# Two context norms made one part sooner, and the second layer's first weights behind the last g, in a two-layer trunk kernel on one core

## The chip, the cores and the metric

The kernel runs on one core of a Trainium2 chip. Its engines each work through a queue of their own, in order: TensorE (PE, matmuls, with PEld for its weight loads), VectorE (DVE), ScalarE (ACT), GpSimd (POOL) and SyncE (SP, which issues DMAs). The metric is the device time of one execution in microseconds (us), lower is better.

## What is computed

The reference is a trunk of two layers over 512 latent tokens x and 256 context tokens c, model width 1024. Layer 0 mixes differential attention and neighbourhood attention, layer 1 is windowed grouped-query attention; each is followed by a SwiGLU FFN. In front of each of the four sub-layers stands a modulated RMS norm, behind each a gated residual add, with separate modulation rows for x and for the context:

```python
def rmsnorm(x, g):
    xf = x.astype(jnp.float32)
    y = xf * lax.rsqrt(jnp.mean(xf * xf, axis=-1, keepdims=True) + NORM_EPS)
    return (y * g.astype(jnp.float32)).astype(x.dtype)

def modulate(h, shift, scale):
    return h * (1 + scale) + shift

def swiglu(h, w1, w3, w2):
    return (jax.nn.silu(h @ w1) * (h @ w3)) @ w2
```

## The kernel before

Everything lies with the model dimension on the 128 partitions: the residual of x is eight tiles `xr[k]` of 512 columns, that of the context eight tiles `cr[k]` of 256. Every operand is kept as a high and a low half, and each product is three matmuls per 128 rows: weight high by h high (L207), weight high by h low (L208), weight low by h high (L209); the FFN's pair products and its down projection do the same on L1233 to L1235 and L1265 to L1267. A weight comes as one DMA of 512 KB from SP into one of three raw buffers. Its halves are made in one of two ways: ACT copies the high half and DVE subtracts (`split`, and L158 and L159 for plain weights), or ACT writes the negated weight, POOL issues a DMA that accumulates the raw weight onto it, and ACT copies the high half (`split_by_dma`).

A norm is a chain over four engines: eight squares on ACT (L329, L332), summed in two accumulators by DVE (L338) and POOL (L336); matmuls with a matrix of ones that sum over the partitions (L309, in `rstd_of`); logarithm, exponential and a Newton step on ACT and DVE (L313 to L318); then for each k the normed and modulated h, DVE (L350), ACT (L351, its high half) and DVE (L352, its low half), in `h_make`. The h's go to `hb[k]`, x columns and context columns apart (`hx`, `hc`). The norm takes its small tiles from a pool or from a `Carve`, which cuts them out of one big tile.

The first attention (until about 478 us) ends with the output projection, whose last context parts are `held` back behind the start of the x norm of the first FFN. The first FFN (478 to 1023 us) begins with `plain_tile(0)`, one hidden tile of 128 columns: two weights by x and by the context, then Silu on ACT, a product on DVE, and the split into `g`. In it `between()`, which is `norm_c`, traces the context norm behind the first x product. `keep_busy` issues 16 matmuls of no use ahead of it. Three more plain tiles follow, then pairs of hidden tiles by a scheme of seven products on token sums (`token_sums`, `seven`). The last pair's down projection is `down_last`: four parts of w2, x columns first (512 wide, eight output tiles m), then the context's 256 columns m by m; behind context m = 2 stands `next_norm`, the x norm of the second attention. The rows of the modulation are made beside this on DVE from streamed weights (L269, L270). The second attention begins with `k_x(0)`, the first K product of x; the context norm of this layer is traced behind it, then V of x and of the context, K of the context, and `k_x(1)`.

What sets the order: the code is traced in this order, and a scheduler then orders each engine's queue by a simulated timeline of its own; `tc.issue_after(a)` holds an instruction behind a in the order. Weights are taken from the stream `S` by `S.next`, which makes the halves of some parts ahead of their use.

## Time and profile before

| what | us |
|---|---|
| median of the runs shown (1660.72 to 1665.11) | 1663.11 |
| the profiled execution | 1662.13 |
| its span | 1660.3 |
| PE busy in the span | 1573.4 |
| DVE busy | 1255.2 |
| ACT busy | 754.0 |
| POOL busy | 270.1 |
| mean granted clock of TensorE | 0.988 |

The profiled execution lies 1.0 us below the median, and 1.8 us of it lie outside the span. PE is busy in 95% of the span, and the chain of work that ended last is PE in 61%. A granted clock of 1.00 is 2.4 GHz, 0.50 is 1.2 GHz; a number between them in a window is a mean of the two.

### The profile page before, as it was taken

Reading aid. Unit: us, or ns where it says so; the run is one execution under the profiler, and the core shown is the slowest. Engines: PE = TensorE matmul, PEld = TensorE weight load, DVE = VectorE, ACT = ScalarE, POOL = GpSimd, SP = SyncE. Lnnn points to the kernel's source line nnn. Section 1 sums busy time; section 2 is a strip of 40 time slices with the busy share of each in tenths; the row PEclk is TensorE's granted clock in tenths of the full one; section 3 lists DMA queues with packets and bytes.
Section 4 is the critical chain, followed back from the end, with each engine's and each line's share of the span. In section 5 each row is a group of like instructions: output and inputs, shape, how many; then the busy total and the mean of one; then the engine's idle time right before and its main releaser. Section 6 shows DMA issues by size and latency. Waiting matters only on the chain.

```text
span 1660.3 us, 26333 instructions
## 1 busy us (share of the span) xinstructions
PE 1573.4 (95%) x10220; PEld 1406.1 (85%) x10220; DVE 1255.2 (76%) x2155; ACT 754.0 (45%) x1330; POOL 270.1 (16%) x314
## 2 busy tenths in 40 slices
PE   5899998999998999999999999999999899999996
PEld 3798987877887889999999987777788798989896
DVE  4758698966565988879798868687666797868685
ACT  5445555456245423333434253456654453524343
POOL 2223112454010000010100011254321000000001
PEclk9999999999999999999999999999999999999998
DMA  9312254544124556675766763411011342323321
GB/s 337 111 56 80 77 156 143 180 140 126 56 82 101 149 167 153 165 199 156 193 186 175 197 167 101 99 54 39 14 39 41 114 138 77 117 87 102 115 77 51
DMA packets 69652, 200.05 MB, mean 120 GB/s; under 512 B 6948, under 2 KB 19396, under 8 KB 69528
## 3 DMA queue, kind: packets, MB, share of 16 engines
q1 hardware_dynamic: 59464, 164.40, 31.8%
q0 software_dynamic: 9488, 33.44, 9.3%
q8 instruction: 81, 1.33, 0.3%
q10 hardware_dynamic: 576, 0.52, 0.1%
q14 instruction: 43, 0.35, 0.1%
HBM read 160.45 MB, written 4.86 MB: 100 GB/s over the span
## 4 chain that ended last, share of the span: by engine, by line
PE 61%; DVE 8%; DMA 4%; issue 3%; ACT 2%; POOL 0%; DVEq 0%; SPq 0%; ACTq 0%; POOLq 0%
PE f L1235 4%; PE f L1234 4%; PE f L1233 4%; PE f L1631 4%; PE f L1633 4%; PE f L1632 4%; PE f L1265 3%; PE f L1266 3%; PE f L1267 3%; PE lin L207 2%; PE t L1466 2%; PE lin L208 2%; PE lin L209 2%; PE f L1686 2%; PE f L1684 2%
## 5 line engine op out<-in xcount | busy, mean ns | idle before, releaser
L196 ACT ACTIVATE wh<-raw 128x1024 fp32r<-128x1024 f32 (+1 forms) x94 | 90.2, 976 | 229.3 <-DVE raw L500 121.1
L207 PE MATMUL lin<-hb,wh 128*128 128x512 f32 (+1 forms) x456 | 162.1, 356 | 8.3 <-DVE q L369 2.2
L208 PE MATMUL lin<-hb,wh 128*128 128x512 f32 (+1 forms) x456 | 160.0, 351 | 0.2
L209 PE MATMUL lin<-hb,wl 128*128 128x512 f32 (+1 forms) x456 | 158.9, 349 | 0.0
L197 DVE TENSOR_TENSOR wl<-raw,wh 128x1024 fp32r<-128x1024 f32 (+1 forms) x94 | 104.5, 1116 | 32.5 <-ACT wh L196 31.8
L159 DVE TENSOR_TENSOR wl<-raw,wh 128x1024 fp32r<-128x1024 f32 x64 | 84.3, 1317 | 41.2 <-ACT wh L158 41.0
L1265 PE MATMUL f<-g,wh 128*128 128x512 f32 (+1 forms) x320 | 108.7, 342 | 5.5 <-DVE q L1247 3.9
L269 DVE SCALAR_TENSOR_TENSOR junk<-raw,tables 128x1024 bf16<-128x1024 f32 x80 | 97.9, 1224 | 17.0 <-DMA raw<-in_ada_wT_dram 16.6
L1267 PE MATMUL f<-g,wl 128*128 128x512 f32 (+1 forms) x320 | 107.5, 341 | 3.3 <-DMA wl<-raw 3.3
L202 POOL DMA_DIRECT2D wl<-raw x42 | 36.6, 872 | 451.0 <-ACT wl L201 409.5
L1266 PE MATMUL f<-g,wh 128*128 128x512 f32 (+1 forms) x320 | 109.3, 342 | 0.0
L207 PEld LDWEIGHTS lin<-hb,wh 128*128 128x128 f32 x456 | 86.4, 190 | 22.8 <-issue 3.0
L1631 PE MATMUL f<-hb,wh 128*128 128x256 f32 x360 | 102.2, 285 | 1.0 <-DVE ns_v L314 1.0
L1632 PE MATMUL f<-hb,wh 128*128 128x256 f32 x360 | 102.2, 284 | 0.0
L1633 PE MATMUL f<-hb,wl 128*128 128x256 f32 x360 | 101.7, 284 | 0.0
L158 ACT CAST wh<-raw 128x1024 fp32r<-128x1024 f32 x64 | 66.9, 1047 | 76.3 <-PE lin L208 22.8
L1233 PE MATMUL f<-hb,wh 128*128 128x384 f32 x288 | 96.4, 335 | 1.8 <-ACT hb L196 1.8
L1234 PE MATMUL f<-hb,wh 128*128 128x384 f32 x288 | 96.3, 334 | 1.1 <-DVE hb L197 1.1
L1235 PE MATMUL f<-hb,wl 128*128 128x384 f32 x288 | 96.2, 334 | 0.0
L208 PEld LDWEIGHTS lin<-hb,wh 128*128 128x128 f32 x456 | 86.7, 190 | 11.2 <-issue 0.9
L209 PEld LDWEIGHTS lin<-hb,wl 128*128 128x128 f32 x456 | 86.6, 190 | 10.5 <-issue 0.3
L336 POOL TENSOR_TENSOR ns_a<-ns_a,ns_s 128x256 f32<-128x256 f32 (+1 forms) x16 | 14.5, 909 | 448.5 <-ACT ns_s L332 446.6
(382 smaller groups left out, 4936.6 us busy)
## 6 DMA issues: line engine op xcount, KB each, us to landing
raw<-in_w_dram SPq DMA_DIRECT2D x132, 512.0 KB, 3.8
raw<-in_ada_wT_dram SPq DMA_DIRECT2D x80, 512.0 KB, 4.2
wl<-raw POOLq DMA_DIRECT2D x42, 512.0 KB, 6.4
raw<-in_w_ab_dram SPq DMA_DIRECT2D x24, 512.0 KB, 4.1
raw<-in_ada_w_dram SPq DMA_DIRECT2D x16, 512.0 KB, 9.3
k<-k SPq DMA_DIRECT2D x16, 384.0 KB, 5.9
raw<-in_w_c_dram SPq DMA_DIRECT2D x12, 512.0 KB, 4.6
nb<-in_na_bias_dram POOLq DMA_DIRECT2D x16, 256.0 KB, 3.8
```

Of the source, the lines that this page charges most:

```text
L207: nc.tensor.matmul(ps, wh(k), xh(k), start=k == 0, stop=False)
L208: nc.tensor.matmul(ps, wh(k), xl(k), start=False, stop=False)
L209: end = nc.tensor.matmul(ps, wl(k), xh(k), start=False, stop=k == n - 1)
L1233: nc.tensor.matmul(ps, wh(k), b[:, 0, :], start=k == 0, stop=False)
L1234: nc.tensor.matmul(ps, wh(k), b[:, 1, :], start=False, stop=False)
L1235: nc.tensor.matmul(ps, wl(k), b[:, 0, :], start=False, stop=k == 3)
L1265: nc.tensor.matmul(ps, hi, g[:, 0, cols[v]], start=first, stop=False)
L1266: nc.tensor.matmul(ps, hi, g[:, 1, cols[v]], start=False, stop=False)
L1267: nc.tensor.matmul(ps, lo, g[:, 0, cols[v]], start=False, stop=last)
L1631: nc.tensor.matmul(ps, wh(k), b[:, 0, :], start=k == 0, stop=False)
L1632: nc.tensor.matmul(ps, wh(k), b[:, 1, :], start=False, stop=False)
L1633: nc.tensor.matmul(ps, wl(k), b[:, 0, :], start=False, stop=k == 3)
```

## The change

The diff, cut to its core:

```diff
-    def last_parts(raw):
+    def last_parts(raw, i):
...
-        split_by_dma(hi, lo, raw[0])
+        (split if i == 1 else split_by_dma)(hi, lo, raw[0])
...
+    g_made = []
+
+    def behind_g(raw):
+        hi, lo = S.part_tiles()
+        with tc.issue_after(g_made[0].ins):
+            nc.scalar.copy(hi, raw[0])
+        with tc.issue_after(g_made[1].ins):
+            nc.vector.tensor_sub(lo, raw[0], f32(hi))
         return hi, lo
...
-            S.add_made([w2[0, j * P : (j + 1) * P, :]], dma_parts if i < 2 else last_parts)
+            S.add_made([w2[0, j * P : (j + 1) * P, :]], (lambda raw, i=i: last_parts(raw, i)) if i else dma_parts)
+
+        for j in (8, 10):
+            S.add_made([w_c[j]], behind_g)
+        for j in (11, 9, 0, 1, 2, 3, 4, 5, 6, 7):
+            S.add(w_c[j])
...
         for m, w in held:
             wo_chunk(m, w, "c", 4)
+        nmap = PoolMap(
+            ns_a0=(sp, "k1", 2), ns_a1=(sp, "k1", 2), ns_s=(sp, "v", 2), ns_h=(sp, "q", 2),
+            ns_v=(sp, "k1", 2), ns_y=(sp, "k2", 1), ns_t=(sp, "v", 2),
+        )
+        r = rstd_of(tp(), sq_sum(cr, nmap), D, nmap)
+        for k in range(KT):
+            act = h_make(k, hc[k], cr[k], r, 0, 1, 1, nmap)
+        silu_tables = act_tables("silu_and_others", act)
...
-        def norm_c():
-            pool = norm_tiles()
-            r = rstd_of(fps(), sq_sum(cr, pool), D, pool)
-            for k in range(KT):
-                act = h_make(k, hc[k], cr[k], r, 0, 1, 1, pool)
-            act_tables("silu_and_others", act)
...
-            pool = norm_tiles()
-            r = rstd_of(fps(), sq_sum(xr, pool), D, pool)
+            t = [apool.tile([P, 1024], F32, tag="ada", name="norm") for _ in range(2)] + [csr[1]]
+            pool = Carve([half(z, i) for z in t for i in range(2)])
+            r = rstd_of(fps(), sq_sum(xr, pool, apart=True), D, pool)
...
-
-            for j in (8, 10, 11, 9, 0, 1, 2, 3, 4, 5, 6, 7):
-                S.add(w_c[j])
...
-                        if not c and not i:
-                            between()
...
+                if j == 0:
+                    with tc.issue_after(silu_tables.ins):
+                        nc.scalar.activation(z[:, cols[c]], ps[0][c], AF.Silu)
...
                 if m == 2:
                     next_norm()
+            q = q_tile()
+            pool = Carve([q[:, NC * i : NC * i + NC] for i in range(6)])
+            r = rstd_of(fps(), sq_sum(cr, pool), D, pool)
+            for k in range(KT):
+                h_make(k, hc[k], cr[k], r, 1, 0, 1, pool)
...
-                    end = split(g[:, 0, :], g[:, 1, :], q)
+                    g_made[:] = [nc.scalar.copy(g[:, 0, :], q), nc.vector.tensor_sub(g[:, 1, :], q, f32(g[:, 0, :]))]
+                    end = g_made[1]
...
         k_x(0, w0)
-        r = rstd_of(linp(), sq_sum(cr, npool), D, npool)
-        for k in range(KT):
-            h_make(k, hc[k], cr[k], r, 1, 0, 1, npool)
```

In words. The first FFN's context norm is traced at the end of the first attention, behind the held context parts, in tiles of that attention's pool; the table of Silu is loaded behind its last activation, and the first tile's Silu is held behind that load. Of w2's last four parts the second is split by ACT and DVE into a big tile. The first two parts of w_c (8 and 10) are held behind the two halves of g on ACT and DVE, and all of w_c is queued in the stream sooner. The x norm of the second attention uses tiles of the modulation's pool, and its eighth square goes to PE as a third source (`apart`). That layer's context norm is traced at the end of `down_last`, ahead of `k_x(0)`. Behind the change the lines of the FFN stand some 16 higher: L1265 to L1267 are L1281 to L1283, L1259 is L1275.

DVE's queue at the end of the first attention and the start of the first FFN, before (res_82 is the context's last residual, hb0 to hb2 the h's of x):

```order
L1053 SCALAR_TENSOR_TENSOR res_82<-lin_4781,mod0_116,res_82 128x256
L318 SCALAR_TENSOR_TENSOR ns_y_4671<-ns_t_4672,ns_y_4671 128x512
L159 TENSOR_TENSOR wl_5039<-raw_4876,wh_5038 128x1024
L350 SCALAR_TENSOR_TENSOR ns_h_4679<-res_4075,amod0_118,ns_y_4671 128x512
L350 SCALAR_TENSOR_TENSOR ns_h_4683<-res_4104,amod0_118,ns_y_4671 128x512
L350 SCALAR_TENSOR_TENSOR ns_h_4687<-res_4185,amod0_118,ns_y_4671 128x512
L352 SCALAR_TENSOR_TENSOR hb0_124<-ns_h_4679,mod0_116,hb0_124 128x512
L352 SCALAR_TENSOR_TENSOR hb1_125<-ns_h_4683,mod0_116,hb1_125 128x512
L350 SCALAR_TENSOR_TENSOR ns_h_4691<-res_4214,amod0_118,ns_y_4671 128x512
L352 SCALAR_TENSOR_TENSOR hb2_126<-ns_h_4687,mod0_116,hb2_126 128x512
```

and after:

```order
L1069 SCALAR_TENSOR_TENSOR res_82<-lin_4781,mod0_116,res_82 128x256
L318 SCALAR_TENSOR_TENSOR ns_y_4671<-ns_t_4672,ns_y_4671 128x512
L159 TENSOR_TENSOR wl_5057<-raw_4943,wh_5056 128x1024
L338 TENSOR_TENSOR ns_a_4796<-ns_a_4796,ns_s_4812 128x256
L350 SCALAR_TENSOR_TENSOR ns_h_4679<-res_4075,amod0_118,ns_y_4671 128x512
L350 SCALAR_TENSOR_TENSOR ns_h_4683<-res_4104,amod0_118,ns_y_4671 128x512
L350 SCALAR_TENSOR_TENSOR ns_h_4687<-res_4185,amod0_118,ns_y_4671 128x512
L338 TENSOR_TENSOR ns_a_4796<-ns_a_4796,ns_s_4815 128x256
L352 SCALAR_TENSOR_TENSOR hb0_124<-ns_h_4679,mod0_116,hb0_124 128x512
L352 SCALAR_TENSOR_TENSOR hb1_125<-ns_h_4683,mod0_116,hb1_125 128x512
L352 SCALAR_TENSOR_TENSOR hb2_126<-ns_h_4687,mod0_116,hb2_126 128x512
```

Two adds of context squares (L338) now stand in it; the four of before stood behind the last x h.

ACT's queue around the last g, before (T_9221 is w2's last part, wh_9541 the high half of w_c's first part):

```order
L201 ACTIVATE T_9221<-raw_9215 128x1024
L203 CAST T_9221<-raw_9215 128x1024
L158 CAST wh_9541<-raw_9535 128x1024
L196 ACTIVATE g_8946<-q_8947 128x1536
L329 ACTIVATE T_9381<-res_4075 128x512
```

and after (T_9237 is w2's last part, wh_9606 and wh_9610 are w_c's first two):

```order
L201 ACTIVATE T_9237<-raw_9231 128x1024
L203 CAST T_9237<-raw_9231 128x1024
L1355 CAST g_8964<-q_8965 128x1536
L532 CAST wh_9606<-raw_9241 128x1024
L532 CAST wh_9610<-raw_9602 128x1024
L329 ACTIVATE norm_9399<-res_4075 128x512
```

The cast of w_c's first part and g have changed places.

PE's queue at the turn from the down projection to the second attention, before (f is the down projection's last context tile, t_9555 is `k_x(0)`, t_9660 and t_9710 are V of x):

```order
L1265 MATMUL f_9485<-g_8946,T_9221 128x256
L1266 MATMUL f_9485<-g_8946,T_9221 128x256
L1267 MATMUL f_9485<-g_8946,T_9221 128x256
L207 MATMUL t_9555<-hb0_124,wh_9541 128x512
L396 MATMUL t_9660<-wh_9545,hb0_124 128x256
L396 MATMUL t_9710<-wh_9545,hb0_124 128x256
L208 MATMUL t_9555<-hb0_124,wh_9541 128x512
```

and after (t_9620 is `k_x(0)`, q_9518 holds the context's squares):

```order
L1281 MATMUL f_9504<-g_8964,T_9237 128x256
L1282 MATMUL f_9504<-g_8964,T_9237 128x256
L1283 MATMUL f_9504<-g_8964,T_9237 128x256
L309 MATMUL f_9519<-q_9518,ones_96 128x256 x2
L207 MATMUL t_9620<-hb0_124,wh_9606 128x512
L208 MATMUL t_9620<-hb0_124,wh_9606 128x512
L209 MATMUL t_9620<-hb0_124,wl_9607 128x512
```

The matmuls on the context's squares now stand ahead of `k_x(0)`; of before they stood behind V of x. DVE's queue there, after, whose last row is the last add of those squares:

```order
L1275 SCALAR_TENSOR_TENSOR res_82<-f_9504,mod0_116,res_82 128x256
L159 TENSOR_TENSOR wl_9615<-raw_9604,wh_9614 128x1024
L350 SCALAR_TENSOR_TENSOR norm_9400<-res_4185,amod1_119,csr1_4883 128x512
L352 SCALAR_TENSOR_TENSOR hb1_125<-norm_9400,mod1_117,hb1_125 128x512
L338 TENSOR_TENSOR q_9518<-q_9518 128x256
L350 SCALAR_TENSOR_TENSOR norm_9400<-res_4214,amod1_119,csr1_4883 128x512
L352 SCALAR_TENSOR_TENSOR hb2_126<-norm_9400,mod1_117,hb2_126 128x512
L338 TENSOR_TENSOR q_9518<-q_9518 128x256
```

Between the last context residual (L1275) and that add stand a subtraction of w_c's third part and six rows that make x h's and add squares.

## Rows read from the trace of the kernel before

**Rows 1.** Windows by stage: busy us (and instructions) of PE, PEld, DVE, ACT, POOL; clock; DMA
```profile
530.00:585.00 55.00, 47.56 (x276) 43.06 (x274) 48.63 (x88) 23.80 (x36) 4.32 (x5) 0.97 0.60 158
...
700.00:800.00 100.00, 100.00 (x577) 95.84 (x576) 84.61 (x144) 35.91 (x40) 7.02 (x9) 1.00 0.68 184
...
1024.00:1059.00 35.00, 29.95 (x197) 27.43 (x198) 26.24 (x46) 17.33 (x34) 5.31 (x6) 0.95 0.15 48
```

**Rows 2.** PE's timeline at the first FFN's context columns: start us, us, what, idle before, releaser
```profile
499.66 1.02 PE L309 MATMUL f<-T,ones 128*128 128x256 f32 x4
...
505.40 1.01 PE L207 MATMUL f<-hb,wh 128*128 128x256 f32 x3 [4.72 <-ACT hb L351]
```

**Rows 3.** Windows of PE behind that gap: busy us, granted clock (1.00 is 2.4 GHz), DMA
```profile
504.00:506.00 2.00, 0.60 (x3) 0.50 0.00 0
506.00:508.00 2.00, 2.00 (x11) 0.50 0.00 0
508.00:510.00 2.00, 2.00 (x13) 0.61 0.00 0
```

**Rows 4.** Timeline at the first FFN's start: PE, then DVE's add of context squares
```profile
478.54 3.73 PE L217 MATMUL f<-ones,ident 128*128 128x128 f32 x32
...
483.87 0.51 PE L208 MATMUL f<-hb,wh 128*128 128x512 f32 x1 [0.27 <-DVE hb L352]
...
492.16 0.42 DVE L338 TENSOR_TENSOR T<-T 128x256 f32<-128x256 f32 x1 [0.17 <-ACT T L332]
```

**Rows 5.** Timeline of POOL and DVE in the second attention
```profile
1038.75 1.29 POOL L379 TENSOR_TENSOR ru<-ru,tables 128x512 f32<-128x512 f32 x1 [1.23 <-DVE ru L377]
...
1039.16 1.16 DVE L338 TENSOR_TENSOR ns_a<-ns_a,ns_s 128x256 f32<-128x256 f32 x1
```

**Rows 6.** Last down projection: timelines of PE, ACT, DVE, then windows of PE
```profile
993.19 1.22 PE L1267 MATMUL f<-g,wl 128*128 128x512 f32 x4 [1.97 <-DMA wl<-raw]
...
993.85 1.05 ACT L158 CAST wh<-raw 128x1024 fp32r<-128x1024 f32 x1 [1.77 <-DMA raw<-in_w_c_dram]
...
994.93 1.23 DVE L159 TENSOR_TENSOR wl<-raw,wh 128x1024 fp32r<-128x1024 f32 x1 [10.64 <-ACT wh L158]
...
994.00:996.00 2.00, 2.00 (x7) 0.56 1.01 158
996.00:998.00 2.00, 2.00 (x7) 0.59 0.89 285
```

**Rows 7.** PE's timeline from the down projection into the second attention, then windows of PE
```profile
1015.22 1.98 PE L309 MATMUL f<-T,ones 128*128 128x512 f32 x4 [0.67 <-DVE T L338]
...
1024.11 0.50 PE L207 MATMUL t<-hb,wh 128*128 128x512 f32 x1 [0.57 <-ACT hb L351]
...
1043.86 1.02 PE L309 MATMUL lin<-ns_a,ones 128*128 128x256 f32 x4
...
1048.32 0.39 PE L396 MATMUL t<-wh,hb 128*128 128x256 f32 x1 [3.44 <-ACT hb L351]
...
1058.70 0.28 PE L209 MATMUL t<-hb,wl 128*128 128x256 f32 x1
1058.82 0.40 PE L207 MATMUL t<-hb,wh 128*128 128x512 f32 x1
1059.06 0.40 PE L208 MATMUL t<-hb,wh 128*128 128x512 f32 x1
...
1048.00:1050.00 2.00, 1.67 (x7) 0.71 0.00 0
1050.00:1052.00 2.00, 2.00 (x12) 0.50 0.00 0
```

**Rows 8.** Timelines of ACT and DVE around the second attention's first h's
```profile
1022.39 1.05 ACT L158 CAST wh<-raw 128x1024 fp32r<-128x1024 f32 x1 [3.13 <-PE f L1266]
...
1040.35 0.42 ACT L332 ACTIVATE ns_s<-res 128x256 f32<-128x256 f32 x1 [2.38 <-DVE ns_a L338]
...
1025.12 0.74 DVE L352 SCALAR_TENSOR_TENSOR hb<-T,mod,hb 128x512 fp32r<-128x512 f32 x1
```

More of the change, by code (lines that the diff above doesn't have):

```diff
@@ L518, in dma_parts @@
         return hi, lo
-    def last_parts(raw):
+    def last_parts(raw, i):
         t = tpool[0]().rearrange("p a b n -> p (a b n)")
         hi, lo = t[:, 0:1024], t[:, 1024:2048]
-        split_by_dma(hi, lo, raw[0])
+        (split if i == 1 else split_by_dma)(hi, lo, raw[0])
+        return hi, lo
+    g_made = []
[5 more added lines that the diff above has]
+            nc.vector.tensor_sub(lo, raw[0], f32(hi))
         return hi, lo
@@ L1116, in tile_trunk, with __init__ @@
         class Carve:
-            def __init__(self, t, **tags):
-                self.t, self.tags = t, tags
+            def __init__(self, places):
+                sq = [2, 3]
+                self.places = places
+                self.tags = dict(ns_a0=[0], ns_a1=[1], ns_s=sq, ns_h=sq, ns_v=[4], ns_y=[5], ns_t=[0])
             def tile(self, shape, dtype, tag, name, **kw):
@@ L1124, in tile @@
                 turn.append(turn.pop(0))
-                return self.t[:, NX * turn[-1] : NX * turn[-1] + shape[-1]]
-        def norm_tiles():
-            sq = [2, 3]
-            return Carve(f32(t_tile()).rearrange("p a b n -> p (a b n)"), ns_a0=[0], ns_a1=[1], ns_s=sq, ns_h=sq, ns_v=[4], ns_y=[5], ns_t=[0])
+                return self.places[turn[-1]]
         def rows(n, after):
@@ L1199, in tile_trunk, with plain_tile @@
         gt = {}
-        def plain_tile(j, g, between=None):
+        def plain_tile(j, g):
             ps = [(fps(), fps()[:, 0:NC]) for _ in range(2)]
             gt[j] = g[:, :, NT * (j % 2) : NT * (j % 2) + NT]
-            if between:
+            if j == 0:
                 keep_busy(ps[0][0], 16, before[0])
@@ L1219, in plain_tile @@
             for c in range(2):
-                nc.scalar.activation(z[:, cols[c]], ps[0][c], AF.Silu)
+                if j == 0:
+                    with tc.issue_after(silu_tables.ins):
+                        nc.scalar.activation(z[:, cols[c]], ps[0][c], AF.Silu)
+                else:
+                    nc.scalar.activation(z[:, cols[c]], ps[0][c], AF.Silu)
             for c in range(2):
@@ L1310, in tile_trunk @@
                     for i in range(2):
-                        end = plain_tile(2 * p + i, g, None if p or i else norm_c)
+                        end = plain_tile(2 * p + i, g)
                         if p:
```

## The prediction

> **What bounds the kernel now.** I read first the windows by stage. In the first FFN's middle TensorE (PE) is busy in all of 100 us, while VectorE (DVE) is busy in 85 and ScalarE (ACT) in 36; in 530 to 585 it is DVE that is nearly full, 48.6 of 55 us, and PE 47.6; around the turn from the first FFN to the second attention, 1024 to 1059, PE has 30.0 of 35 us [rows 1]. So time is to be had only where PE stands still, and where a standstill is followed by matmuls at a lower clock. The timeline of PE shows three such places near the code that the change touches: 4.72 us before the context columns of the first FFN's first tile, released by ACT's first context h [rows 2]; 1.97 us inside the last down projection, released by an accumulating DMA [rows 6]; 3.44 us inside the second attention's K and V products, released by ACT's first context h again [rows 7]. Behind each the granted clock falls to 0.50, the 1.2 GHz level, for some us [rows 3, 6, 7]. A last look went to what stands in the queues of ACT and DVE at those places, in the order of the changed program.
>
> **Part A, context norm of the first FFN.** It goes from behind the first x tile to the end of the first attention. Removed: the 4.72 us of standstill [rows 2], and the slow matmuls behind it. In 505.4 to 510 the clock is 0.50, 0.50 and 0.61 [rows 3], so 0.6 x 0.50 + 2 x 0.50 + 2 x 0.39 = 2.1 us are lost. The two matmuls of ones on the squares, 1.02 us [rows 2], leave this place too. Together 7.8 us.
> Added, in front of x: the context's adds. Two of the four stand in DVE's queue between the rows that make the first x h's, 2 x 0.42 = 0.84 us [rows 4], in a stretch where DVE runs without a gap; the other two fall where it waits for PE's residuals. The matmuls on the squares now stand in PE's queue behind the third x matmul, where PE already waits 0.27 us for DVE [rows 4], so they cost 1.02 - 0.27 = 0.75 us. The later steps (three of 0.42 us for the root, and the context h's behind the x h's) hold back x's last h by 1.3 us, which PE, busy with two x tiles until 499.66, does not meet. Tables: ACT loads fewer activation tables there, and those on the way to the context's h's lie inside the 4.72 us already counted; the one that is left stands ahead of the first tile's Silu, whose columns nobody needs before the down projection. Sum for A: -7.8 + 0.84 + 0.75 = **-6.2 us**. The stretch 530 to 585, where DVE is the bound, starts with the last product of tile 1 and so moves with it; behind it PE is full [rows 1], so I let the whole gain pass to the end. Bounds: -7 (the two added terms hidden) and -1.7 (rival 1).
>
> One row speaks against putting these adds there. While POOL ran a tensor op of 1.29 us, a DVE add that takes 0.42 us elsewhere took 1.16 us [rows 4, 5], 0.74 us more. Two of the context's adds are POOL's, and they now run beside DVE's dense stretch, so up to 2 x 0.74 = 1.5 us could be added to A; I take none of it, since their turn comes while DVE still waits for residuals. The Trainium skill, page "GPSIMD Engine Reference", section "1. Specifications", says that GpSimd shares its SBUF interfaces with VectorE and contends with DVE instructions that have two SBUF inputs; by that rule A would be -4.7 instead of -6.2, and the trace agrees that the collision exists, with 0.74 us for it.
>
> **Part B, the last down projection and the second attention.** Three edits act together.
> First, w2's second part is split by ACT and DVE instead of by ACT and a DMA. The 1.97 us wait goes [rows 6], and the slow matmuls behind it: (0.44 + 0.41) x 2 = 1.7 us [rows 6]. The last g's low half is then needed sooner; today ACT's copy of it stands behind the cast of the first w_c part, which waits 1.77 us for its DMA, and DVE's half behind w_c's subtraction, which waited 10.64 us [rows 6]. The change turns this order round, so g comes about 2.5 us sooner; I leave 0.6 us of a new wait there. The 512-column part of the down projection thus ends about 3 us sooner.
> Second, DVE's residuals follow g, so x's squares go to PE as much sooner as g does, about 2.8 us ahead of 1015.22, at 1012.4. They come as three sources instead of two (one PE source more, one DVE add less): 1.98 us become some 2.7, since passes overlap. 60 context matmuls at 0.12 us follow, to 1022.3, where they end at 1023.5 today (1024.11 - 0.57) [rows 7].
> Third, the context norm of the second attention stands ahead of its first K product instead of behind it, and that is a new wait. PE's row has the two matmuls on the context's squares before k_x(0), and the last of these squares stands behind work for x: on ACT behind the cast of w_c's third part, which waits for PE's last context matmul to give back a weight tile, then an x h, then the squares of 0.42 us; on DVE behind that part's subtraction and the first x h's. By rows that is 1.05 (cast) + 1.23 (subtraction) + 4 x 0.74 (h's halves) + 2 x 0.42 (adds) = 6.1 us, less some 0.3 by which such rows overlap [rows 4, 6, 8]: 5.8 us, in which PE does nothing. Then 1022.3 + 5.8 + 1.0 (the squares' matmuls) = 1029.1 for k_x(0), five us later than today's 1024.11. Queued behind the waiting matmul are all K and V products, so nothing fills the gap, and I count the slow clock at 2.1 us, as after the 4.72 us gap.
> What it buys: from there PE runs through k_x(0) and four V tiles of x, 24 x 0.24 + 96 x 0.12 = 17.3 us, and finds the context h's made: today the first comes 4.5 us behind the squares' matmuls (1043.86 to 1048.32), here five x h's of two halves of 0.74 us stand between, so the first is there at about 1041, while PE asks for it at 1048. So 8.6 us (72 x 0.12) for the context's V and K follow without the 3.44 us and without the slow windows of 0.71 and 0.50 there, 1.6 us [rows 7]. The second K product, k_x(1), starts at 1029.1 + 2.1 + 17.3 + 8.6 = 1057.1, against 1058.82 today [rows 7]: **-1.7 us**. Bounds: -5 if the chain on ACT and DVE is met by half, +2 if x's h's hold PE at the low clock for 4 us more.
>
> The rest: w_c's later parts keep their place; at the start of the second FFN the same matmuls stand in another order, with the same ACT and DVE rows, which I cost at 0 +- 0.5. Sum: 1662.1 - 6.2 - 1.7 = 1654.2 us for the profiled execution (its span 1660.3 and 1.8 around it). The median shown is 1.0 us above it, so the forecast is **1655 us**. The kernel's own runs spread such that about 0.3% (5 us) can be told from no change.
>
> **Rivals.**
> (1) A is mostly swallowed at its new place. For: DVE has no gap where the first x h's are made, and the POOL collision is in the trace. If each add waits for its square as today, they take 3.3 us instead of 0.84, PE stands before the first tile long enough for the low clock, and A is -6.2 + 2.5 + 2.0 = -1.7; with B 1663.1 - 3.4 = 1659.7. By the POOL collision alone it is 1656.6. Against: PE's keep-busy matmuls cover 3.73 us there [rows 4], and the squares have the residuals' time to run in.
> (2) B's new wait costs more than the one removed. For: the chain runs over three engines. If x's h's delay the last squares by two more pairs (4 x 0.74 = 3.0 us), B is +1.3 and the time 1658.2.
> (3) Slower. Mechanism: behind the new wait at the context's squares PE takes k_x(0) no faster than DVE makes h's, in pieces with small gaps, and the clock stays at 0.50 through all of the x work. Price: 17.3 us instead of 2.1, so B is +13.5 and the time 1663.1 - 6.2 + 13.5 = 1670. It ends slower than before once PE spends more than some 12 us of full-speed work at 0.50 there. Against: today the clock comes back after 4 to 5 us with the same kind of feed [rows 3, 7].
> (4) The change does not do what it says: g still waits, because on ACT two casts for w2's last part stand ahead of it and need a DMA that lands about 990. Then the first edit of B loses 1 to 2 us, which the new wait at the squares hides: 1655 to 1656, inside the forecast.
>
> **How the numbers follow.** Forecast (with 4 in it) 0.62, own range 1651.5 to 1657.5; rival 1 0.20; rival 2 0.09; rival 3 0.09. The range over all reaches from 1651.5 (A -7, B -5) to 1661 (rival 1 with a median's scatter); rival 3 and a little below are left out. Faster by over 0.3% (below 1658.1) is the forecast and a part of rival 2: 0.65; within 0.3% the rest of 1 and 2: 0.26; slower 0.09.
>
> **What would show it.** In the changed profile: no gap over 1 us on PE in 483 to 525 and a clock of 1.00 there; tile 1's last g 6 to 7 us sooner; no DMA wait at L1283 (today's L1267) near 993; a PE gap of 5 to 6 us before k_x(0) with a clock of 0.50 behind it; no gap at the context's V. I am wrong if x's first matmul of the first FFN moves by over 2 us, if the gap before k_x(0) is under 3 or over 9 us, or if the stretch 530 to 585 grows by what came before it.

## The result and the profile after

The changed kernel takes 1656.6 us (median of 11 runs, 1652.2 to 1661.6) where the kernel before takes 1666.4 on the same chip: a ratio of 0.9946, 95% interval 0.9932 to 0.9961, some 9 us. Timed once more beside a later experiment it was 0.9953 (0.9937 to 0.9969). The forecast was 1655.0 us with a range of 1651.5 to 1661.0, and faster by over 0.3% as the likeliest. It counted from 1663.1 us, so the gain that it forecast is 8.1 us; measured are some 9, with an interval of 6.5 to 11.3.

| what | before | after |
|---|---|---|
| profiled execution, us | 1662.13 | 1656.03 |
| its span | 1660.3 | 1654.3 |
| PE, DVE, ACT, POOL busy | 1573.4, 1255.2, 754.0, 270.1 | 1571.1, 1251.8, 750.2, 270.7 |
| mean granted clock | 0.988 | 0.989 |

The engines do almost the same work; what has gone is time in which PE stood or ran slowly.

**First FFN.** PE's timeline of the changed kernel (start us, us, what, count, idle before and its releaser): the keep-busy matmuls, the first x product with the two matmuls on the context's squares in it, and the passage from x columns (512 wide) to context columns (256 wide), which answers to [rows 2, 4].

```profile
478.68 3.73 PE L217 MATMUL f<-ones,ident 128*128 128x128 f32 x32
...
483.27 0.97 PE L207 MATMUL f<-hb,wh 128*128 128x512 f32 x3 [0.86 <-ACT hb L351]
484.17 1.13 PE L309 MATMUL t<-ns_a,ones 128*128 128x256 f32 x4
...
499.71 0.40 PE L209 MATMUL f<-hb,wl 128*128 128x512 f32 x1
499.94 0.28 PE L208 MATMUL f<-hb,wh 128*128 128x256 f32 x1
```

The 4.72 us gap is gone and nothing stands in its place. Windows of the changed kernel, with the columns of [rows 1], answer to [rows 3, 1, 6, 7]: 

```profile
504.00:506.00 2.00, 2.00 (x17) 1.91 (x16) 0.35 (x1) 1.43 (x3) 0.00 (x0) 1.00 0.00 0
506.00:508.00 2.00, 2.00 (x16) 1.87 (x15) 1.21 (x2) 2.00 (x3) 0.00 (x0) 1.00 0.23 16
...
1024.00:1059.00 35.00, 33.71 (x222) 31.22 (x223) 22.13 (x41) 14.93 (x26) 2.58 (x2) 0.95 0.20 65
994.00:996.00 2.00, 2.00 (x10) 1.67 (x9) 2.00 (x4) 0.00 (x0) 0.00 (x0) 1.00 0.79 219
...
1024.00:1026.00 2.00, 0.71 (x2) 0.62 (x3) 2.00 (x5) 0.79 (x2) 0.00 (x0) 0.74 0.92 371
1026.00:1028.00 2.00, 2.00 (x6) 1.56 (x5) 1.97 (x4) 1.25 (x3) 0.00 (x0) 0.50 0.00 0
1028.00:1030.00 2.00, 2.00 (x9) 1.64 (x8) 2.00 (x6) 1.83 (x4) 0.00 (x0) 0.91 0.00 0
```

The clock is 1.00 behind 504, where it was 0.50 for two windows, and 1.00 at 994, where it was 0.56. In 1024 to 1059 PE now has 33.7 us of 35 instead of 30.0, but that flatters the change: of the new wait of 5.50 us, shown below, 4.2 us lie ahead of 1024. The slow windows have not left this stage either: they stand at its start, 1024 to 1030, and the row at 1026 with six matmuls at 0.50 is the trace of the new wait.

**What the first part brought, and where it is met.** Low half of tile 1's last g on DVE, and the first matmul of the second down projection on PE, in the timeline of before:

```profile
527.83 0.96 DVE L197 TENSOR_TENSOR g<-q,g 128x768 fp32r<-128x768 f32 x1 [2.16 <-ACT g L196]
...
584.88 0.80 PE L1265 MATMUL f<-g,wh 128*128 128x512 f32 x1 [3.85 <-DVE q L1247]
```

The same two in the changed kernel:

```profile
520.68 0.96 DVE L197 TENSOR_TENSOR g<-q,g 128x768 fp32r<-128x768 f32 x1 [2.16 <-ACT g L196]
...
577.84 0.79 PE L1281 MATMUL f<-g,wh 128*128 128x512 f32 x1 [4.81 <-DVE q L1263]
```

They are 7.15 and 7.04 us sooner. PE's wait there, which DVE's q ends, grows from 3.85 to 4.81, but that q is sooner too, so it costs no more than 0.1 of the lead. A cleaner mark is the first product that is 384 columns wide, as both kernels do the same 384 matmuls (192 on x, 192 on the context) between the keep-busy matmuls and it. In before, then in the changed kernel:

```profile
557.64 0.39 PE L1233 MATMUL f<-hb,wh 128*128 128x384 f32 x1
...
551.18 0.34 PE L1249 MATMUL f<-hb,wh 128*128 128x384 f32 x1
```

Counted from the keep-busy matmuls (478.54 and 478.68) these are 79.1 and 72.5 us, 6.6 us less. Tile 1's last g gains 0.7 us more than that, as in before four matmuls of the next tile stand ahead of tile 1's last ones.

**Second attention.** Timeline of the changed kernel: the last g on ACT and DVE with the casts of w_c behind it, then PE from the sum of x's squares to k_x(0). These answer to [rows 6, 7].

```profile
988.04 1.47 ACT L1355 CAST g<-q 128x1536 fp32r<-128x1536 f32 x1
989.41 1.99 ACT L532 CAST wh<-raw 128x1024 fp32r<-128x1024 f32 x2
989.54 1.76 DVE L1355 TENSOR_TENSOR g<-q,g 128x1536 fp32r<-128x1536 f32 x1 [8.25 <-ACT g L1355]
...
1009.77 2.84 PE L309 MATMUL f<-norm,ones 128*128 128x512 f32 x6 [3.16 <-DVE norm L338]
...
1025.29 2.07 PE L309 MATMUL f<-q,ones 128*128 128x256 f32 x4 [5.50 <-DVE q L338]
1026.81 0.99 PE L207 MATMUL t<-hb,wh 128*128 128x512 f32 x1
```

The g comes ahead of w_c, as the change wants it. Two waits are new. One was not forecast: PE waits 3.16 us for the sum of x's squares (`norm,ones`), where before it waited 0.67 [rows 7]. In the second profile of the changed kernel this wait is 2.67 us, and there the clock falls behind it, so that the sum takes 4.54 us instead of 2.84. The sum's row there, and the windows behind the wait in the first and in the second profile:

```profile
1007.36 4.54 PE L309 MATMUL f<-norm,ones 128*128 128x512 f32 x6 [2.67 <-DVE norm L338]
...
1010.00:1012.00 2.00, 2.00 (x5) 0.83 (x5) 1.32 (x4) 1.20 (x3) 0.00 (x0) 1.00 0.00 0
...
1008.00:1010.00 2.00, 2.00 (x4) 0.74 (x3) 0.91 (x3) 0.94 (x3) 0.00 (x0) 0.50 0.00 0
```

All kernels below with the changed part B have this wait, 1.9 to 3.2 us; with the order of before it is 0.5 to 1.9. Seven of the context's matmuls, 0.84 us, now stand behind this sum instead of ahead of it; what else makes DVE's last add late was not tested.

The other new wait is the forecast one: the context's sum (`q,ones`) makes PE wait 5.50 us. DVE's timeline up to 1025.29 shows why:

```profile
1019.83 0.48 DVE L1275 SCALAR_TENSOR_TENSOR res<-f,mod,res 128x256 f32<-128x256 f32 x1
1020.23 1.22 DVE L159 TENSOR_TENSOR wl<-raw,wh 128x1024 fp32r<-128x1024 f32 x1
1021.36 1.22 DVE L350 SCALAR_TENSOR_TENSOR norm<-res,amod,csr 128x512 f32<-128x512 f32 x1
1022.50 0.74 DVE L352 SCALAR_TENSOR_TENSOR hb<-norm,mod,hb 128x512 fp32r<-128x512 f32 x1
1023.16 0.41 DVE L338 TENSOR_TENSOR q<-q 128x256 f32<-128x256 f32 x1
1023.50 0.74 DVE L350 SCALAR_TENSOR_TENSOR norm<-res,amod,csr 128x512 f32<-128x512 f32 x1
1024.16 0.74 DVE L352 SCALAR_TENSOR_TENSOR hb<-norm,mod,hb 128x512 fp32r<-128x512 f32 x1
1024.82 0.41 DVE L338 TENSOR_TENSOR q<-q 128x256 f32<-128x256 f32 x1
```

The context's last residual is there at 1020.3. Then DVE takes a weight's subtraction and two x h's before the last two of the context's adds: DVE is not idle, but PE needs the rows at the end of its queue. The row at 1021.36 takes 1.22 us where the same kind of row at 1023.50 takes 0.74, and POOL's add of context squares runs beside it:

```profile
1020.69 1.34 POOL L336 TENSOR_TENSOR q<-q 128x256 f32<-128x256 f32 x1 [4.70 <-ACT q L332]
```

That is the collision of POOL and DVE that the prediction weighed for part A; here it is 0.5 us of the 5.50, and the second profile has it too (1.21 us).

### The profile page after: what moved, and what is told of

Its sections match the earlier page's. It is cut to its first block, busy times and chain, and to the rows that moved or that the text cites. A ratio compares the mean times of both kernels' runs of the same rounds, so it can differ in the third digit from the quotient of the medians.

```text
span 1654.3 us, 26329 instructions
## 1 busy us (share of the span) xinstructions
PE 1571.1 (95%) x10222; PEld 1404.2 (85%) x10222; DVE 1251.8 (76%) x2155; ACT 750.2 (45%) x1326; POOL 270.7 (16%) x313
## 4 chain that ended last, share of the span: by engine, by line
PE 62%; DVE 6%; DMA 5%; ACT 2%; issue 2%; POOL 0%; DVEq 0%; SPq 0%; ACTq 0%; POOLq 0%
PE f L1251 4%; PE f L1250 4%; PE f L1249 4%; PE f L1650 4%; PE f L1652 4%; PE f L1651 4%; DMA wl<-raw 3%; PE f L1281 3%; PE f L1282 3%; PE f L1283 3%; PE f L207 3%; PE f L208 2%; PE f L209 2%; PE lin L207 2%; PE t L1485 2%; PE lin L208 2%
## 5 line engine op out<-in xcount | busy, mean ns | idle before, releaser
L1281 PE MATMUL f<-g,wh 128*128 128x512 f32 (+1 forms) x304 | 103.5, 342 | 8.1 <-DVE q L1263 4.8
L159 DVE TENSOR_TENSOR wl<-raw,wh 128x1024 fp32r<-128x1024 f32 x62 | 81.2, 1309 | 31.0 <-ACT wh L158 28.2
L1282 PE MATMUL f<-g,wh 128*128 128x512 f32 (+1 forms) x304 | 103.3, 341 | 0.0
L1283 PE MATMUL f<-g,wl 128*128 128x256 f32 (+1 forms) x304 | 101.8, 338 | 0.8 <-DMA wl<-raw 0.8
L1251 PE MATMUL f<-hb,wl 128*128 128x384 f32 x288 | 96.5, 335 | 0.8 <-DMA wl<-raw 0.6
```

The source lines that it names most:

```text
L1251: nc.tensor.matmul(ps, wl(k), b[:, 0, :], start=False, stop=k == 3)
L1281: nc.tensor.matmul(ps, hi, g[:, 0, cols[v]], start=first, stop=False)
L1282: nc.tensor.matmul(ps, hi, g[:, 1, cols[v]], start=False, stop=False)
L1283: nc.tensor.matmul(ps, lo, g[:, 0, cols[v]], start=False, stop=last)
```

## Experiments

Times against the kernel before, in four groups, each beside runs of before on its own chip; and, from each one's single profiled execution, the length of three stages as a difference to the first profile of before: from the FFN's keep-busy matmuls to its second down projection (106.3 us there), from that to the last down projection (397.8), and from that to the first score matmul of the second attention (96.5).

| kernel | median us | ratio (95%) | to 2nd down | middle | to scores |
|---|---|---|---|---|---|
| changed | 1656.6 | 0.9946 (0.9932 to 0.9961) | -7.2 | +4.0 | -2.8 |
| changed, again | 1655.5 | 0.9953 (0.9937 to 0.9969) | -6.7 | +2.7 | -1.3 |
| before, again | 1663.6 | 0.9993 (0.9981 to 1.0005) | +1.0 | +0.4 | +1.1 |
| a_alone | 1657.9 | 0.9959 (0.9945 to 0.9973) | -6.6 | +1.4 | -1.7 |
| b_alone | 1656.9 | 0.9956 (0.9942 to 0.9970) | +0.2 | -0.7 | -6.2 |
| hold11 | 1655.0 | 0.9940 (0.9927 to 0.9953) | -6.8 | +0.5 | -2.0 |
| busy | 1652.8 | 0.9927 (0.9913 to 0.9941) | -7.0 | +2.9 | -2.0 |
| hold_busy | 1650.2 | 0.9917 (0.9900 to 0.9934) | -6.1 | +0.8 | -5.2 |
| no_e | 1653.5 | 0.9928 (0.9908 to 0.9947) | -7.4 | +1.2 | -6.5 |
| no_e, again | 1649.5 | 0.9915 (0.9894 to 0.9935) | -6.7 | +0.8 | -6.0 |
| no_c | 1657.0 | 0.9952 (0.9935 to 0.9970) | -6.5 | +0.1 | -1.4 |
| no_d | 1654.4 | 0.9938 (0.9920 to 0.9956) | -6.9 | +2.2 | 0.0 |
| fill_a | 1662.7 | 0.9984 (0.9971 to 0.9996) | -0.8 | +2.7 | -0.7 |

**The two parts alone.** a_alone is the kernel before with the first FFN's context norm moved, and the load of the Silu table with it, and nothing else; b_alone is the changed kernel with that move undone (the norm's small tiles then lie in one T tile).

```diff
 a_alone, on the kernel before
...
+        r = rstd_of(tp(), sq_sum(cr, nmap), D, nmap)       # behind the held output chunks
+        for k in range(KT):
+            act = h_make(k, hc[k], cr[k], r, 0, 1, 1, nmap)
...
-                        if not c and not i:
-                            between()
 b_alone, on the changed kernel: the same lines the other way round
```

> The kernel before with part A alone: the context norm of the first FFN made at the end of the first attention, the second layer untouched. Theory (A is worth its whole place): the gap of 4.72 us and the slow clock behind it go, tile 1's last g is about 7 us sooner as in the changed kernel, and the whole passes to the end: 6 us below the kernel before, ratio 0.996. Rival (A is given back later in the FFN, as the trace of the changed kernel, where its lead falls from 7.0 us at the second down projection to 3.0 us at the last, could mean): 3 us below, ratio 0.998.

> The changed kernel with part A undone: the first FFN's context norm stands behind the first x tile again (in a T tile, as before), all edits of the last down projection and the second attention stay. Theory: only B's terms are left, the DMA wait of 1.97 us and the two slow stretches gone, the new gap of 5.5 us there: 1.7 to 3 us below the kernel before, ratio 0.998 to 0.999. Rival (A is given back): B must hold the rest of the 9 us, so 5 to 6 us below, ratio 0.9965.

a_alone is 6.8 us faster than before (0.0041 x 1665), as its theory said; b_alone is 7.3 us faster, more than either of my two figures for it. The two together gain only 8 to 9, so part B on top of part A is worth 1 to 2 us, which the intervals do not tell from none. The profile of b_alone says where the overlap is; it is no overlap at all. PE there, from the first matmul of k_x(0):

```profile
1021.45 0.39 PE L207 MATMUL t<-hb,wh 128*128 128x512 f32 x1
...
1025.13 0.50 PE L208 MATMUL t<-hb,wh 128*128 128x512 f32 x1 [1.50 <-DVE hb L352]
```

There is no 5.50 us wait. Both kernels trace the context norm at the same place of the code, but the scheduler put the context's sum elsewhere: on PE's queue it stands right ahead of k_x(0) in the changed kernel, 30 matmuls behind its first one in b_alone, and 120 behind it in the kernel before and in a_alone. So b_alone is not the changed kernel's part B, and a_alone, which keeps the 120, has the old wait at the context's V. Its PE rows, the first of them from the last down projection:

```profile
990.01 0.50 PE L1270 MATMUL f<-g,T 128*128 128x512 f32 x1 [1.29 <-DVE g L197]
...
1041.08 0.38 PE L396 MATMUL t<-wh,hb 128*128 128x256 f32 x1 [3.44 <-ACT hb L351]
```

**What the new wait is made of.** hold11 holds the halves of w_c part 11 (the L159 at 1020.23 above, and its cast on ACT) behind the context's last square and add; busy puts 24 keep-busy matmuls on PE ahead of the context's sum and leaves the wait as it is.

```diff
 hold11, on the changed kernel
+        with tc.issue_after(sq_made[0].ins):
+            nc.scalar.copy(hi, raw[0])
+        with tc.issue_after(sq_made[1].ins):
+            nc.vector.tensor_sub(lo, raw[0], f32(hi))
...
-        for j in (11, 9, 0, 1, 2, 3, 4, 5, 6, 7):
+        S.add_made([w_c[11]], behind_sq)
+        for j in (9, 0, 1, 2, 3, 4, 5, 6, 7):
 busy, on the changed kernel
-            r = rstd_of(fps(), sq_sum(cr, pool), D, pool)
+            ps = fps()
+            accs = sq_sum(cr, pool)
+            keep_busy(ps, 24)
+            r = rstd_of(ps, accs, D, pool)
```

> The changed kernel, with the third part of w_c (11) held behind the context's last square on ACT and behind its last add on DVE. Theory (the 5.5 us gap before the context's sum is the chain through that part's cast and subtraction and two x h's): the gap falls to about 2.6 us (residual 0.4, square and adds 1.0, two steps of x h's 1.3), the slow clock behind it goes with it: 3 to 5 us below the changed kernel, ratio to the kernel before 0.992. Rival (the x h's, not the cast, set the wait, or k_x(0) then waits for x h's that come later): the gap falls but K stands still behind it, 0 to 1 us below the changed kernel, ratio 0.9945.

> The changed kernel with 24 matmuls of no use (ones by identity, 128 columns, some 5.6 us) ahead of the context's sum, where PE stands still for 5.5 us. Theory (the clock falls because PE stands still): the clock stays at 1.00 from 1020 to 1034, the 1.6 us lost there come back, the sum starts within 0.3 us of where it did: 1 to 1.6 us below the changed kernel, ratio to the kernel before 0.9937. Rival (the clock there is not set by the gap): the windows behind it still show 0.50 to 0.74, the time is as the changed kernel's or above by what the filler overruns, ratio 0.9946 to 0.995.

PE's row of the context's sum in hold11:

```profile
1021.12 2.08 PE L309 MATMUL f<-q,ones 128*128 128x256 f32 x4 [3.48 <-DVE q L340]
```

In busy, PE's timeline with the fillers and the sum:

```profile
1019.21 5.52 PE L219 MATMUL f<-ones,ident 128*128 128x128 f32 x48
1024.87 1.13 PE L309 MATMUL f<-q,ones 128*128 128x256 f32 x4
```

And busy's window of the stage, columns as in [rows 1]:

```profile
1024.00:1059.00 35.00, 34.82 (x241) 32.13 (x240) 23.11 (x43) 14.74 (x26) 3.10 (x3) 1.00 0.24 69
```

Holding the weight's two rows back takes 2.0 us off the 5.50, not the 2.9 that I expected, and the sum still takes 2.08 us, so the slow clock stayed. With the fillers the sum takes 1.13 us instead of 2.07 and the clock is 1.00 through the stage. By the times this is worth some 3 us (0.9927 against 0.9946), though the intervals overlap, and the stage in its profile, -2.0, lies between the changed kernel's -2.8 and -1.3; hold11's 1 us can't be told from none.

**Both together** (16 fillers, since the wait is shorter).

> The changed kernel with both single edits at the start of the second attention: the halves of w_c part 11 held behind the context's last square and its last add (it shortened the gap ahead of the context's sum from 5.50 to 3.48 us), and keep-busy matmuls in that gap, 16 of them (24 kept the clock at 1.00 there). Theory: the two savings are of different things, one of the wait's length, one of the clock behind it, and add up. Against before, hold11 has 0.9940 and busy 0.9927 where the changed kernel has 0.9946, so the sum is 0.9921, some 1651.7 us where before takes 1664.85. Rival: the fillers already cover the stretch that the shorter gap saves, as PE's next work waits for something else: as busy alone, 0.9927, 1652.7 us. Second rival: 16 fillers end before the sum is ready and the clock falls again: as hold11, 0.9940.

PE's timeline of hold_busy at the sum:

```profile
1017.75 3.73 PE L219 MATMUL f<-ones,ident 128*128 128x128 f32 x32
1021.40 1.13 PE L309 MATMUL f<-q,ones 128*128 128x256 f32 x4
1022.18 0.58 PE L207 MATMUL t<-hb,wh 128*128 128x512 f32 x1
```

They show no wait at the sum, and the sum itself takes 1.13 us. The ratio is 0.9917 where the sum of the two savings gave 0.9921, so it fits the first theory, though its interval does not exclude busy's 0.9927. It beats the kernel before surely, and the changed kernel by some 5 us (its interval just reaches that of the changed kernel's first timing, and not that of the second); its stage is 5.2 us shorter than before's.

**One edit of part B undone at a time.**

```diff
 no_e: the context norm of the second attention behind k_x(0) again
-            q = q_tile()
...
-                h_make(k, hc[k], cr[k], r, 1, 0, 1, pool)
...
         k_x(0, w0)
+        r = rstd_of(linp(), sq_sum(cr, npool), D, npool)
 no_c: w2's second part by an accumulating DMA again
-        (split if i == 1 else split_by_dma)(hi, lo, raw[0])
+        split_by_dma(hi, lo, raw[0])
 no_d: w_c parts 8 and 10 not held behind g
-            S.add_made([w_c[j]], behind_g)
+            S.add(w_c[j])
```

> The changed kernel with one edit undone: the context norm of the second attention is traced behind k_x(0) again, as in the kernel before. It tells whether that move is worth anything. Theory (the prediction's sum): the gap of 5.50 us ahead of the context's sum and the half clock behind it (together some 7.6 us) go, and the gap of 3.44 us and its 1.6 us of half clock come back at the context's V (5.0 us): 2 to 3 us faster than the changed kernel, a ratio near 0.993. Rival: the x norm's h's, not the context's sum, are then what PE waits for, so that k_x(0) starts no sooner and the second gap is added: 3 to 5 us slower than the changed kernel, a ratio near 0.997.

> The changed kernel with the context norm of the second attention traced behind k_x(0) again, once more, beside the changed kernel itself: the two differ in that edit alone. Its first look gave 0.9928, with an interval (0.9908 to 0.9947) that reaches the changed kernel's 0.9946. Theory: in the changed kernel the context's sum stands ahead of k_x(0) on PE, which waits 5.50 us for it and then runs at half clock; traced behind, the sum stands 38 rows later and PE waits for the x h's alone, 1.5 us: 0.9925, some 3.5 us faster than the changed kernel. Rival: the first look was luck, the k_x(1) and V behind it wait instead: within 1 us of the changed kernel, 0.994 to 0.995.

> The changed kernel with one edit undone: the second part of w2 in the last down projection has its halves made through an accumulating DMA again. It tells which of the edits took the 1.97 us wait for a DMA away. Theory (the prediction's): this one did; a DMA wait of about 2 us comes back early in the last down projection and the clock falls to 0.50 behind it for 1.7 us: 3 to 4 us slower than the changed kernel, a ratio near 0.9968. Rival: the wait went because the halves of w_c no longer stand ahead of the last g; then no wait comes back and the time is that of the changed kernel, 0.9946.

> The changed kernel with one edit undone: the halves of w_c parts 8 and 10 are ordered freely and not held behind the last g. It tells what holding them is worth. Theory (the prediction's): they stand ahead of the last g on ACT and DVE again, each a cast of about 1.3 us and a subtraction of about 1.3 us; the last g comes some 2.5 us later and PE waits for it: 0 to 2.5 us slower than the changed kernel, a ratio of 0.9946 to 0.996. Rival: what then ends the wait of the context's sum is the DVE work behind the last g, which is 2.6 us shorter for it; the gap of 5.50 us shrinks by as much and the time stays at 0.9946 or falls to 0.993.

no_e is the plain answer to b_alone's question. Its profile, second time, at the x h's and the context's sum:

```profile
1023.47 0.50 PE L208 MATMUL t<-hb,wh 128*128 128x512 f32 x1 [1.50 <-DVE hb L352]
...
1026.96 1.13 PE L309 MATMUL lin<-ns_a,ones 128*128 128x256 f32 x4
```

The sum stands 39 matmuls behind k_x(0)'s first one, finds its squares made, and delays nobody; the 3.44 us wait at the context's V, which my expectation had come back, does not. In the two profiles the stage is 6.5 and 6.0 us shorter than before, as in b_alone (6.2), where the changed kernel has 2.8 and 1.3. In the same group of runs no_e took 1649.5 and the changed kernel 1655.5 us (intervals 0.9894 to 0.9935 and 0.9937 to 0.9969). So the move of the second context norm does not bring a gain; it takes about 4 us by the stage, 3 to 6 by the times, of what the other edits of part B bring.

no_c and no_d settle less. In no_c PE's waits in the last down projection are for g and not for a DMA, so my expectation fell; in no_d PE waits 0.29 us for the last g and not some 2.5, so that one fell too, and the wait at the context's sum stayed at 5.49, so the rival's shrinking gap fell. PE's longest of these waits in no_c:

```profile
987.93 0.50 PE L1282 MATMUL f<-g,T 128*128 128x512 f32 x1 [1.29 <-DVE g L1355]
```

And in no_d:

```profile
1023.40 2.07 PE L309 MATMUL f<-q,ones 128*128 128x256 f32 x4 [5.49 <-DVE q L338]
```

Their times (0.9952, 0.9938) can't be told from the changed kernel's. What each of these two edits is worth by itself stays open. The x norm's other tiles, its eighth square as a third source and the earlier queueing of w_c were not undone by themselves at all, so which of part B's edits brings its gain is not shown.

**Before and after, once more.**

> The kernel before, once more, for a second profiled execution and as a measure of the comparison itself. Ratio 1.000 within 0.0015. Two things are read from the profile. First, how far the stages of one and the same kernel differ between executions: from the second down projection of the first FFN to the last one, kernels whose code there is the same took 0.1 to 4.0 us longer than the profile of before; if that is the spread of executions, a second profile of before differs from the first by 1 to 2 us there, and if it is what a lead of 7 us brings about, it is the same as the first within 0.5 us. Second, the wait for a DMA of 1.97 us in the last down projection [rows 6], which came back neither in the kernel with the DMA undone nor in the one with part A alone: if it belongs to the order of before it is there again, 1.5 to 2.5 us; if it was that execution's, it is under 0.5 us or the wait is for another engine.

> The changed kernel, once more, on the same chip and in the same minutes as the next one: ratio to before 0.9946 within 0.0015. From its profile: the gap ahead of the context's sum at the second attention's start 5.3 to 5.7 us with the clock at 0.50 behind it, as it hangs on the order alone; the second down projection 6.0 to 7.4 us sooner behind the start of the FFN than in before. From there to the last down projection 4.0 us longer than before if the lead is lost to waits that it makes itself, 0 to 3 if the 4.0 us was that execution's.

PE's waits in the second profile of before, in the last down projection and at the context's V:

```profile
999.94 0.50 PE L1265 MATMUL f<-g,T 128*128 128x512 f32 x1 [1.18 <-ACT g L196]
1001.73 0.80 PE L1266 MATMUL f<-g,T 128*128 128x512 f32 x1 [1.29 <-DVE g L197]
...
1053.02 0.58 PE L396 MATMUL t<-wh,hb 128*128 128x256 f32 x1 [3.44 <-ACT hb L351]
```

The 3.44 is the order's; it is the same to the last digit. The 1.97 us for a DMA [rows 6] is not: this time PE waits for g at that place, 2.5 us in two pieces, after 0.97 us for a DMA earlier. Which cause came last there changed from one execution to the next. The second profile of the changed kernel has its 5.50 us wait at the context's sum again. As to the FFN's middle, where no code differs in what it does, the ten profiles with part A range from +0.1 to +4.0 us and the four without it from -0.7 to +2.7. Two profiles of one kernel differ less there: by 0.4 us (before), 1.3 (the changed kernel) and 0.4 (no_e). By the marks that I had set, before's 0.4 speaks for something that the kernels bring about and the changed kernel's +2.7 for its execution. So the spread is not shown to be that of executions alone, and whether a lead of 7 us adds to it (means 1.7 and 0.6) can't be told from so few.

**The half clock by itself.** fill_a is the kernel before with fillers in the 4.72 us gap.

```diff
                 for c in range(2):
+                    if c:
+                        keep_busy(ps[0][1], 28, sum_made[0])
```

> The kernel before with 28 keep-busy matmuls (3.3 us at 2.4 GHz) behind the context's sum in the first FFN, in the gap of 4.72 us at 505.40 [rows 2]; the norm stays where it was. It measures one term of the prediction's part A by itself, the half clock behind the gap [rows 3], put at 2.1 us. Theory: the gap itself stays (its end hangs on the context's norm), the clock is 1.00 behind it, and everything behind comes 2.1 us sooner: 1662.7 us where before takes 1664.8, a ratio of 0.9987, and the second down projection 2.1 us sooner behind the start of the FFN. Rival: part A's gain is all from the gap and the moved matmuls, the work behind the gap being held by the g's of the tile anyway: 0, a ratio of 1.000.

The number of fillers was a mistake of mine: 16 of them show as 32 rows in 3.73 us [rows 4], so 28 take 6.42 us, not 3.3, and outlast the gap. PE's timeline of fill_a, with the first context matmul and the first 512-wide one behind the context's:

```profile
497.23 6.42 PE L217 MATMUL f<-ones,ident 128*128 128x128 f32 x56
503.40 0.48 PE L207 MATMUL f<-hb,wh 128*128 128x256 f32 x2
...
512.11 0.40 PE L207 MATMUL f<-hb,wh 128*128 128x512 f32 x1
```

One of its windows behind the gap:

```profile
506.00:508.00 2.00, 2.00 (x19) 2.00 (x18) 1.82 (x5) 1.05 (x3) 0.00 (x0) 1.00 0.00 0
```

The same 512-wide matmul on PE's timeline of before, where the context starts at 505.40 [rows 2]:

```profile
515.94 0.40 PE L207 MATMUL f<-hb,wh 128*128 128x512 f32 x1
```

The stretch, 72 context matmuls in both, takes 8.7 us at a clock of 1.00 and 10.5 at the clocks of [rows 3]: the term is 1.8 us, against 2.1 in the prediction. The time, 0.9984, is not told from before's own second 0.9993: the fillers that outlast the gap give 1.3 us of the 1.8 back. That the ratio meets the 0.9987 of the expectation confirms nothing, as that number stood on the wrong length of the fillers.

## Why the prediction was right, and where it was not

**Part A, -6.2 us: right, with the additions too high.** Alone it measured -6.8 us (0.9959, interval -9.2 to -4.5). The gap of 4.72 went whole and the clock stayed at 1.00, as said; no wait over 0.86 us stands in 483 to 525. The half clock is 1.8 and not 2.1. From the keep-busy matmuls to the first product of 384 columns the changed kernel takes 6.6 us less (all ten profiles with part A have 72.5 us there), where gap, the squares' matmuls and clock make 4.72 + 1.02 + 1.83 = 7.6. So the additions cost 1.0 us and not 1.59. Of the adds, put at 0.84, PE sees 0.49: it waits 0.86 us for the first x h instead of 0.37. The squares' matmuls hold x's next matmul up by 0.78 (484.17 to 484.95) and the wait of 0.27 is gone, so they cost 0.5 and not 0.75. The collision with POOL was rightly left out here: POOL's last add of context squares ends at 478.8, DVE makes its first x h at 481.7, and DVE's two adds there take 0.41 us each. It came in the second attention instead, where the prediction had no term for it (0.5 us, above).

**"I let the whole gain pass to the end."** Counted from the keep-busy matmuls the lead is 7.2 us at the second down projection; at the last one the first profile has 3.1, and I first took that for a lead that is given back. In no_c, with the same code there, the lead is 6.5 and then 6.4. The timed ratio of a_alone says that the gain passes, within its interval.

**Part B, -1.7 us: the sum came out by luck, as two of its terms are wrong and their errors cancel.** Most of the timelines came as drawn: no DMA wait near 993, a gap of 5.50 us before the context's sum (5.8), a clock of 0.50 behind it for some 3 us, no gap at the context's V. The stage is 2.8 and 1.3 us shorter in two profiles; against the mean of the four profiles with before's order there (0, +1.1, -1.7, -0.7; -0.3) that is -1.7, but those four lie 2.8 us apart, so that the agreement is no closer than a us or two. The second step left a wait out. X's squares are on PE 2.5 us sooner behind the last down projection's start, as said (2.8), but x's columns there end 4.1 us sooner, and a part of that goes into the wait of 3.16 us (2.67 in the second profile), which the prediction put at nothing; the squares' matmuls take the 2.7 us of the prediction only where the clock holds (2.84 and 4.54). The step "what it buys" is wrong. It credited the moved context norm with the 3.44 us wait and the slow windows behind it, 5.0 us. no_e and b_alone lose that wait without paying for it: with the other edits in place the scheduler sets the context's sum 30 to 39 matmuls behind k_x(0)'s first one instead of 120, and it neither holds PE up there nor comes too late. So the other edits are worth about -6 us, not the -4.6 that the sum leaves for them (-1.7 - 2.9), and the move costs about +4, where I had it at 5.8 + 2.1 - 5.0 = +2.9 but as the necessary price of the gain. A part of the -4.6 stands in the sum unnamed: it runs k_x(0) and x's V tiles through in 17.3 us, where before takes 19.8 (1024.11 to 1043.86) with waits of 1.07 and 0.22 us for x's h's; in the changed kernel these waits are gone. I had read the order of before and of the changed kernel, and compared only these two places, too late and too early; the place between was not among the rivals.

The first edit's reason was weak too. It took the wait there for the DMA's alone. Of the other three profiles with that order, two show a wait for g in its place, and fill_a one of 1.64 us for the DMA and then 1.09 for g.

**Start of the second FFN, 0 +- 0.5.** The squares' matmuls there take 2.08 and 1.96 us in the changed kernel's two profiles, 1.18 and 1.69 in those of before, and the next x product is 0.3 to 0.9 us later. By the end it has come back: from the first score matmul on the changed kernel takes 581.0 and 580.9 us, before 581.2 and 581.8. Nothing of it shows in the time.

**Rivals.** 1 (A swallowed at its new place) fell with a_alone. 2 is half true: its two more pairs of x h's did not come (5.50 us, not 8.8), but the new wait does cost more than the move removes; part B as a whole is not slower for it. 3 (half clock through all of the x work, 1670 us) fell: the clock is 0.91 again in 1028 to 1030, and 0.99 there in the second profile. 4 is half true: ACT's copy of g does stand behind two casts for w2, the first of which waits 6.3 us for its DMA, but g is ready sooner than before relative to the down projection, and PE did not wait for it in the first profile and 0.36 us in the second.

## What to carry to other kernels

When a chain's result is made sooner, ask where its consumer stands in the in-order queue. There is a window between "too early, the engine stands in front of it" and "too late, the next user waits for what it feeds", and a scheduler can move the consumer by tens of matmuls for a change elsewhere (here from right ahead of k_x(0) to 30 matmuls behind it for a norm 500 us earlier): read that place in the order for the whole change and for each part alone. Parts whose gains don't add up in the times need not share a bottleneck; the part alone may be another program. And where a wait can't be removed, fillers that end just before it does kept the clock here (hold_busy); those that outlast it cost what they outlast it by (fill_a, 1.3 us).

## What the runs showed of the hardware that was not expected

One execution's waits are not the kernel's: at the same place PE waited 1.97 us for a DMA in one profile of the same program and 2.5 us for ACT and DVE in the next, and 400 us of code that does the same differed by 0.4 to 1.3 us between two profiles of one kernel. Waits that hang on the order alone came back to 0.01 us in the second profiles (3.44, 4.72, 5.50).

The clock followed what PE did just before: behind a wait of 5.50 us the first matmuls ran at 0.50, with 16 to 24 matmuls of no use in the wait at 1.00 and the sum of the context in 1.13 instead of 2.07 us. A shorter wait can go either way in one and the same kernel: behind 3.16 us at x's squares the clock stayed at 1.00, behind 2.67 us in the next profile it fell to 0.50.

A DVE row beside a running POOL add took 1.22 us instead of 0.74, in both profiles of the changed kernel.
